# Layout of the compressed keys' and values' tokens in a hybrid attention block: one row of tokens and a shifted copy, or eight phases

## Chip, core and metric

The kernel runs on one core of a Trainium2 chip. The metric is the device time of one execution in microseconds (us), the median of several executions. The engines: PE (TensorE, matmuls; PEld is its weight load), DVE (VectorE), ACT (ScalarE), POOL (GpSimd), SP (SyncE, which here issues the transfers). A matmul below is written `out<-moving,stationary`.

## What is computed

One decoder layer on 512 tokens of width 1024: two attention branches side by side (differential attention, and sparse attention with compressed, selected and windowed keys), merged by gates, then an MLP. The change touches one step of the sparse branch, the compression of keys and of values:

```python
def compress(kv, pos_emb, w1, w2):            # kv: (1, 512, 4 groups, 64)
    n_cmp = (S - CMP_BLOCK) // CMP_STRIDE + 1 # 31 blocks of 32 tokens, 16 apart
    idx = jnp.arange(n_cmp)[:, None] * CMP_STRIDE + jnp.arange(CMP_BLOCK)[None, :]
    blocks = kv[:, idx] + pos_emb[None, None, :, None, :]
    blocks = blocks.transpose(0, 1, 3, 2, 4).reshape(B, n_cmp, G, CMP_BLOCK * Dh)
    return jax.nn.gelu(blocks @ w1) @ w2      # w1: (2048, 256), w2: (256, 64)
...
k_cmp = compress(kc.reshape(B, S, G, HEAD_DIM), cmp_pos_k[l], cmp_k_w1[l], cmp_k_w2[l])
v_cmp = compress(vc.reshape(B, S, G, HEAD_DIM), cmp_pos_v[l], cmp_v_w1[l], cmp_v_w2[l])
```

## The kernel before

**Tiling.** Every product is float32 made of parts: `split` writes a rounded high part (a cast on ACT or DVE) and a low part (a subtraction on DVE, for weights on DVE or POOL), and three matmuls (high by high, low by high, high by low) stand for one. Activations lie with 128 features or 128 tokens on the partitions; a PSUM bank is 128x512, and a chunk of a projection fills four banks (`gbanks`, four buffers named `gb`). Weights come in pieces of 128x1024 through `WStream`: a transfer into `wraw`, casts into `whi`, subtractions into `wlo`, each with two buffers.

**Order.** One generator, `filler`, walks the plan of matmul chunks (`add(...)`, lines 1556 to 1603): queries and keys of two differential heads, their values, `kc_chunk`, then `weave(diff_chunk(1, True), hidden(0))`, which alternates one weight piece of a projection with one piece of the compression's first layer for keys; then `diff_chunk(2)`, then `weave(dv_chunk(1, True), hidden(1))`, the same for values; and so on to the MLP. Streams for rotary embedding, scores and values of the attention heads run ahead of it in priority. All this only notes instructions. `Sched.flush` then gives each a place by a list schedule with prices and latencies written into the kernel, chooses for each cast or copy between ACT and DVE and for each weight subtraction between DVE and POOL, and emits the order of every engine at line 357, which is why each row below says L357. A change in one place so moves the order everywhere behind it.

**The step.** `kc_chunk` ends with `gb` banks that hold, for 512 tokens, the keys of groups 0 and 1, those of 2 and 3, and the values likewise. `u_split(0, ...)` splits the two key banks, 64 partitions (one group) at a time, into the lower half of the tile `U` (high and low, 2096 columns: four groups of 512 tokens and 48 columns of position embedding). One transfer then writes the upper half: the same columns one token further, so that a matmul contracts over two tokens of 64 features. The value banks are copied to a tile `kk`. In `hidden(kv)`, for each of two column tiles of w1 and each token pair `a` of 16, a matmul reads `U` from column 2a with a step of 16 (130 columns, high and low: 260), and one reads the high part alone (130). When `hidden(0)` is through, `u_split(1, ...)` does for the values what was done for the keys, into the next buffer of the same tag.

Of the kernel before, what the change touches and what calls it, by code (L numbers as in the profile page):

```python
# [11 lines left out]
F32 = mybir.dt.float32  # L12
F32R = mybir.dt.float32r
# [413 lines left out]
def hybrid_block(ctx: ExitStack, tc: tile.TileContext, x, ln_mix_g, w_in, dqg, dkg, lq1, lk1, lq2, lk2,  # L427
# [4 lines left out]
    V, A, P, T, Q = (Engine(sched, n, e) for n, e in (("DVE", nc.vector), ("ACT", nc.scalar), ("POOL", nc.gpsimd),  # L432
                                                      ("PE", nc.tensor), ("SP", nc.sync)))
# [3 lines left out]
    def pool(stack, name, space="SBUF"):  # L437
        kw = {} if space == "SBUF" else {"space": getattr(MT, space)}
        return Pool(sched, stack.enter_context(tc.tile_pool(name=name, bufs=1, **kw)), space)
# [10 lines left out]
    def f(ap):  # L450
        return ap.bitcast(F32)
# [4 lines left out]
    def copy(out, src, engs=("ACT", "DVE")):  # L456
        sched.note([(e, COPY[e], getattr(sched.engs[e], COPY[e])) for e in engs], (out, src), {})

    def tt(out, a, b, op, engs=("DVE",)):
        sched.note([(e, "tensor_tensor", sched.engs[e].tensor_tensor) for e in engs], (out, a, b), {"op": op})  # L460

    def split(hi, lo, src, hi_engs=("ACT", "DVE"), lo_engs=("DVE",)):

        copy(hi, src, hi_engs)
        tt(lo, src, f(hi), OP.subtract, lo_engs)
# [60 lines left out]
    def gemm_dm(banks, xs, nk=KT):  # L526

        for kp in range(nk // 2):
            hi, lo = ws.get()
            for a in range(2):  # L530
                kt = kp * 2 + a
                rh, rl = xs(kt)
                for c in range(4):
                    wh = hi[:, a * 512 + c * 128:a * 512 + (c + 1) * 128]
                    wl = lo[:, a * 512 + c * 128:a * 512 + (c + 1) * 128]
                    o = banks[c]
                    if len(rh.shape) == 3:
                        o = o.rearrange("p (t n) -> p t n", t=rh.shape[1])
                    mm(o, wh, rh, 512, kt == 0, False)
                    mm(o, wh, rl, 512, False, False)  # L540
                    mm(o, wl, rh, 512, False, kt == nk - 1)
                    yield 0
# [22 lines left out]
    with ExitStack() as ps:  # L565
# [5 lines left out]
        att = pool(ps, "att")  # L571


        def k_tile(dtype=F32R):
            return att.tile([128, 2, 2, 512], dtype, tag="kk", bufs=3, name="kk")
# [4 lines left out]
        UW = 2096  # L580
# [107 lines left out]
        def gbanks():  # L688
            return [pg.tile([128, 512], F32, tag="g", bufs=4, name="gb") for _ in range(4)]
# [11 lines left out]
        q_slots, k_slots, v_slots, r_slots = Slots(9), Slots(3), Slots(12), Slots(5)  # L701
# [12 lines left out]
        def there(key):  # L714
            if key not in ready:
                ready[key] = When(pe)
            return ready[key]


        U = [None, None]  # L720
        vcraw = [None]

        def u_split(kv, srcs):
            U[kv] = att.tile([128, 2, UW], F32R, tag="big", bufs=1, name="U")
            u = U[kv]

            pp = att.tile([128, 48], F32, tag="pp", bufs=1, name="pp")
            Q.dma_start(pp, (posk, posv)[kv])
            split(u[:, 0, 2048:], u[:, 1, 2048:], pp)
            for c in range(2):  # L730
                for g in range(2):
                    c0 = (c * 2 + g) * 512
                    split(u[0:64, 0, c0:c0 + 512], u[0:64, 1, c0:c0 + 512], srcs[c][g * 64:(g + 1) * 64])
            Q.dma_start(f(u[64:128, :, 0:2047]), f(u[0:64, :, 1:2048]))
            there(("U", kv)).after(9000)

        def kc_chunk():
            banks = gbanks()
            yield from gemm_dm(banks, hxs)
            u_split(0, banks[:2])  # L740
            yield k_slots.can(1)
            k_slots.take(1)
            vcraw[0] = k_tile(F32)[:, 0]
            for c in range(2):
                copy(vcraw[0][:, c, :], banks[2 + c])

        def hidden(kv):
            yield there(("U", kv))
            u = U[kv]
            w2r = att.tile([128, 2, 64], F32, tag="sc", bufs=2, name="w2r")  # L750
            Q.dma_start(w2r, (kw2, vw2)[kv][0].rearrange("(m p) n -> p m n", p=128))
            w2s = att.tile([128, 2, 2, 64], F32R, tag="pc", bufs=4, name="w2s")
            split(w2s[:, :, 0, :], w2s[:, :, 1, :], w2r)
            ghs = []
            for m in range(2):
                yield t_bank()
                hb = ptr.tile([128, 2, 256], F32, tag="t", bufs=2, name="hb")
                for a8 in range(2):
                    hi, lo = ws.get()
                    for aa in range(8):  # L760
                        a = a8 * 8 + aa
                        u2 = u[:, :, 2 * a:2 * a + 16 * 129 + 1:16]
                        c0 = aa * 128
                        mm(hb[:, :, 0:130], hi[:, c0:c0 + 128], u2, 260, a == 0, False)
                        mm(hb[:, 0, 0:130], lo[:, c0:c0 + 128], u2[:, 0, :], 130, False, a == 15)
                    if a8 == 1:
                        t_use(2000)
                    yield PIECE
                hs = att.tile([128, 130], F32, tag="sc", bufs=2, name="hs")
                copy(hs, hb[:, 0, 0:130])  # L770
                V.tensor_tensor(hs, hs, hb[:, 1, 0:130], op=OP.add)
                u_ = att.tile([128, 128], F32, tag="yt", bufs=2, name="hu")
                V.tensor_scalar(u_, hs[:, 0:128], hs[:, 128:129], None, op0=OP.add)
                t3 = att.tile([128, 128], F32, tag="ysq", bufs=2, name="t3")
                V.tensor_tensor(t3, u_, u_, op=OP.mult)
                V.tensor_tensor(t3, t3, u_, op=OP.mult)
                V.scalar_tensor_tensor(t3, t3, 0.044715, u_, op0=OP.mult, op1=OP.add)
                A.activation(t3, t3, AF.Tanh, scale=math.sqrt(2.0 / math.pi))
                V.tensor_scalar(t3, t3, 1.0, 0.5, op0=OP.add, op1=OP.mult)
                V.tensor_tensor(t3, t3, u_, op=OP.mult)  # L780
                gh = att.tile([128, 2, 128], F32R, tag="pc", bufs=4, name="gh")
                split(gh[:, 0, :], gh[:, 1, :], t3)
                ghs.append(gh)
            if kv == 0:
                u_split(1, [vcraw[0][:, c, :] for c in range(2)])
                k_slots.give(1)
            side.append(cmp_out(kv, ghs, w2s))

        def weave(main, sub):
# [349 lines left out]
        big = [None]  # L1139
# [504 lines left out]
```

## Time and profile before

| | |
|---|---|
| median of 3 executions | 1106.4 us (1106.22 to 1110.23) |
| the profiled execution | 1109.28 us |
| its span in the trace | 1107.5 us |
| PE busy | 1061.3 us, 96% |
| DVE / ACT / POOL busy | 769.9 / 462.0 / 490.3 us |
| granted TensorE clock, mean | 0.989 |

The span is what the trace covers; the profiled execution is 1.8 us longer, and 2.9 us above the median. Ends of matmuls in the trace are modelled and overlap, so the pace of PE is read from one start to the next. Busy shares are averages: up to about 700 us the attention streams run beside the projections, afterwards the MLP has PE nearly for itself.

### The profile page before, as it was taken

The page shows a single profiled execution, that of the slowest core. Times are in us where ns is not written, and L with a number is a line of the kernel's source. Part 1 is how long each engine was busy: PE and PEld are TensorE (multiplying, and loading weights), DVE is VectorE, ACT ScalarE, POOL GpSimd, SP SyncE. Part 2 cuts the span into 40 slices and gives each one's busy share as a digit, 9 for nine tenths or more (in the row PEclk, how much of TensorE's full clock was granted, in tenths as well). Part 3 has the DMA queues.
Part 4 walks back from the last instruction along what each step waited for, and adds up shares of the span by engine and source line. Part 5 has one row for each costly group of instructions (what it writes and reads, how often), then busy time and mean ns, then how long its engine had stood idle before and what let it go on. Part 6 is the DMA issues. An engine that isn't in the chain of part 4 may idle for free.

```text
span 1107.5 us, 15713 instructions
## 1 busy us (share of the span) xinstructions
PE 1061.3 (96%) x5257; PEld 881.4 (80%) x5257; DVE 769.9 (70%) x1899; ACT 462.0 (42%) x1125; POOL 490.3 (44%) x485
## 2 busy tenths in 40 slices
PE   6998988999999999998999997999999999999998
PEld 5877867788877788787788885888888888888887
DVE  7678498899888999999999897655543223345232
ACT  4256335566554556655465664213322111233110
POOL 3844698458687381392211213333333222333221
PEclk9999998999999999999999998999999999999999
DMA  6364345642645224454353243632232323332232
GB/s 207 96 171 109 109 128 145 160 149 69 172 121 159 75 66 155 121 189 165 117 178 124 96 153 113 228 105 79 93 103 100 102 96 95 96 95 96 95 133 76
DMA packets 83905, 136.76 MB, mean 123 GB/s; under 512 B 8817, under 2 KB 33905, under 8 KB 83825
## 3 DMA queue, kind: packets, MB, share of 16 engines
q1 hardware_dynamic: 83824, 135.77, 40.3%
q8 instruction: 41, 0.67, 0.2%
q14 instruction: 40, 0.32, 0.1%
HBM read 106.64 MB, written 14.42 MB: 109 GB/s over the span
## 4 chain that ended last, share of the span: by engine, by line
PE 74%; DVE 11%; DMA 6%; POOL 4%; issue 2%; SPq 1%; ACT 1%; DVEq 0%; ACTq 0%; POOLq 0%
PE gb L357 38%; PE ga L357 21%; PE sb L357 4%; PE avn L357 3%; PE ptn L357 3%; DMA kk<-kp 2%; DVE p L357 2%; PE hb L357 2%; POOL wlo L357 1%; PE av L357 1%; DVE st L357 1%; POOL str L357 1%; SPq L357 1%; DVE big L357 1%; POOL t1r L357 1%
## 5 line engine op out<-in xcount | busy, mean ns | idle before, releaser
L357 POOL TENSOR_TENSOR wlo<-wraw,whi 128x512 fp32r<-128x512 f32 (+1 forms) x214 | 305.3, 1436 | 523.4 <-ACT whi L357 350.2
L357 ACT CAST whi<-wraw 128x512 fp32r<-128x512 f32 (+1 forms) x213 | 127.6, 617 | 353.2 <-PE gb L357 172.6
L357 DVE CAST whi<-wraw 128x512 fp32r<-128x512 f32 (+1 forms) x101 | 45.8, 454 | 208.2 <-PE ga L357 96.1
L357 PE MATMUL gb<-wlo,hTh 128*128 128x512 f32 (+2 forms) x352 | 135.4, 386 | 2.8 <-POOL wlo L357 1.5
L357 PE MATMUL gb<-whi,hTl 128*128 128x512 f32 (+2 forms) x352 | 134.6, 383 | 0.0
L357 PE MATMUL gb<-whi,hTh 128*128 128x512 f32 (+2 forms) x352 | 131.1, 392 | 1.8 <-ACT hTh L357 1.2
L357 DVE CUSTOM_DVE_ANT_0 p<-sb,cst 128x512 f32<-128x512 f32 (+2 forms) x192 | 91.7, 480 | 9.6 <-PE sb L357 8.9
L357 DVE TENSOR_TENSOR wlo<-wraw,whi 128x512 fp32r<-128x512 f32 (+2 forms) x100 | 82.7, 828 | 4.8 <-ACT whi L357 0.7
L357 ACT ACTIVATE p<-p,smn 128x512 f32<-128x512 f32 (+3 forms) x128 | 71.9, 562 | 33.1 <-DVE smn L357 32.5
L357 PEld LDWEIGHTS gb<-wlo,hTh 128*128 128x128 f32 x352 | 67.4, 191 | 14.6 <-POOL wlo L357 3.1
L357 PEld LDWEIGHTS gb<-whi,hTh 128*128 128x128 f32 x352 | 67.4, 194 | 13.3 <-ACT hTh L357 1.6
L357 PEld LDWEIGHTS gb<-whi,hTl 128*128 128x128 f32 x352 | 67.3, 191 | 10.2 <-DVE hTl L357 0.3
L357 DVE TENSOR_SCALAR p<-p,smn,gates 128x512 f32<-128x512 f32 (+3 forms) x128 | 68.8, 546 | 0.9
L357 PE MATMUL gb<-big,whi 128*128 128x512 f32 x192 | 67.2, 404 | 0.0
L357 PE MATMUL gb<-hTl,whi 128*128 128x512 f32 x160 | 64.8, 405 | 0.0
L357 DVE TENSOR_TENSOR al<-ptn,ah 128x128 fp32r<-128x128 f32 (+3 forms) x128 | 61.0, 481 | 4.8 <-ACT ah L357 2.2
L357 PE MATMUL gb<-hTh,whi 128*128 128x512 f32 x160 | 64.3, 403 | 0.0
L357 PE MATMUL gb<-hTh,wlo 128*128 128x512 f32 x160 | 63.5, 404 | 0.0
L357 PE MATMUL ga<-h2l,whi 128*128 128x512 f32 x160 | 62.4, 390 | 0.0
L357 PE MATMUL ga<-h2h,whi 128*128 128x512 f32 x160 | 62.4, 391 | 0.0
L357 PE MATMUL ga<-h2h,wlo 128*128 128x512 f32 x160 | 62.3, 389 | 0.0
L357 PE MATMUL ptn<-cst,p 128*128 128x128 f32 x320 | 58.4, 276 | 2.3 <-DVE al L357 0.8
(246 smaller groups left out, 2634.7 us busy)
## 6 DMA issues: line engine op xcount, KB each, us to landing
wraw<-in_w_in_dram SPq DMA_DIRECT2D x36, 512.0 KB, 3.6
wraw<-in_w_mlp_up_dram SPq DMA_DIRECT2D x32, 512.0 KB, 3.9
wraw<-in_w_mlp_down_dram SPq DMA_DIRECT2D x32, 512.0 KB, 3.5
kk<-kp SPq DMA_DIRECT2D x48, 256.0 KB, 4.5
wraw<-in_w_in_dram SPq DMA_DIRECT2D x36, 256.0 KB, 4.1
big<-yd SPq DMA_DIRECT2D x16, 512.0 KB, 3.7
yd<-yo SPq DMA_DIRECT2D x8, 512.0 KB, 3.1
wraw<-in_w_proj_diff_dram SPq DMA_DIRECT2D x8, 512.0 KB, 3.9
```

Of the source, the lines that this page charges most:

```text
L357: op.ways[op.eng][0](*op.a, **op.k)
```

## The change

Both `U` tiles become one tile, `[128, keys or values, high or low, 8 phases of 130 columns]`. Token 16m + 2h + z of a group lies in phase h, column m of its group, and on the lower or upper 64 partitions by z. Sixteen copies (`kk<-gb`, 64 partitions, 8x32 elements) take the four banks out of PSUM into a tile `kk`, reading every sixteenth column of a bank; then casts and subtractions of 128x512 make `U` from `kk`, for keys and for values right behind each other. The matmuls of `hidden` read 130 neighbouring columns from column `a % 8 * 130 + a // 8`. The two transfers `U<-U`, the two whole-bank copies and the second `u_split` behind `hidden(0)` go, and the planner takes `U` for ready after 6000 instead of 9000 of its nanoseconds. The last columns of each part are set to zero.

```diff
-        U = [None, None]
-        vcraw = [None]
-
-        def u_split(kv, srcs):
-            U[kv] = att.tile([128, 2, UW], F32R, tag="big", bufs=1, name="U")
-            u = U[kv]
-
-            pp = att.tile([128, 48], F32, tag="pp", bufs=1, name="pp")
-            Q.dma_start(pp, (posk, posv)[kv])
-            split(u[:, 0, 2048:], u[:, 1, 2048:], pp)
-            for c in range(2):
+        U = [None]
+        UP = 130
+
+        def u_split(srcs):
+            ut = att.tile([128, 2, 2, 8 * UP + 4], F32R, tag="big", bufs=1, name="U")
+            U[0] = ut
+            V.memset(f(ut[:, :, :, 8 * UP:]), 0.0)
+            raw = k_tile(F32).rearrange("p a b n -> p (a b n)").rearrange("p (v h g m) -> p v h g m", v=2, h=8, g=4)
+            for k, src in enumerate(srcs):
+                kv, c = k // 2, k % 2
                 for g in range(2):
-                    c0 = (c * 2 + g) * 512
-                    split(u[0:64, 0, c0:c0 + 512], u[0:64, 1, c0:c0 + 512], srcs[c][g * 64:(g + 1) * 64])
-            Q.dma_start(f(u[64:128, :, 0:2047]), f(u[0:64, :, 1:2048]))
-            there(("U", kv)).after(9000)
+                    for z in range(2):
+                        sv = src[g * 64:(g + 1) * 64].rearrange("p (m h z) -> p z h m", h=8, z=2)[:, z]
+                        copy(raw[z * 64:(z + 1) * 64, kv, :, c * 2 + g, :], sv)
+            for kv in range(2):
+                u = [ut[:, kv, w, 0:8 * UP].rearrange("p (h n) -> p h n", n=UP) for w in range(2)]
+                pp = att.tile([128, 48], F32, tag="pp", bufs=1, name="pp")
+                Q.dma_start(pp, (posk, posv)[kv])
+                split(u[0][:, :, 128:], u[1][:, :, 128:], pp[:, 0:32:2].rearrange("p (z h) -> p h z", z=2))
+                rv = raw[:, kv].rearrange("p h g m -> p h (g m)")
+                for h in (0, 4):
+                    split(u[0][:, h:h + 4, 0:128], u[1][:, h:h + 4, 0:128], rv[:, h:h + 4])
+                there(("U", kv)).after(6000)
...
             yield from gemm_dm(banks, hxs)
-            u_split(0, banks[:2])
             yield k_slots.can(1)
             k_slots.take(1)
-            vcraw[0] = k_tile(F32)[:, 0]
-            for c in range(2):
-                copy(vcraw[0][:, c, :], banks[2 + c])
+            u_split(banks)
+            k_slots.give(1)
...
-            u = U[kv]
+            u = U[0][:, kv]
...
-                        u2 = u[:, :, 2 * a:2 * a + 16 * 129 + 1:16]
+                        at = a % 8 * UP + a // 8
+                        u2 = u[:, :, at:at + 130]
...
-            if kv == 0:
-                u_split(1, [vcraw[0][:, c, :] for c in range(2)])
-                k_slots.give(1)
```

What it moves on three engines is shown next. A number behind a name tells buffers apart.

PE, where the first piece of `hidden(0)` stands; `gb_341` to `gb_344` are the banks of `diff_chunk(1)`, `whi_314` its first weight piece, `whi_361` its second. Before:

```order
L357 MATMUL gb_344<-whi_314,hTl_69 128x512
L357 MATMUL av_354<-vt_234,ah_349 128x256
L357 MATMUL av_354<-vt_234,al_350 128x256
L357 MATMUL gb_341<-whi_361,hTh_68 128x512
L357 MATMUL gb_342<-whi_361,hTh_68 128x512
L357 MATMUL gb_343<-whi_361,hTh_68 128x512
L357 MATMUL gb_344<-whi_361,hTh_68 128x512
L357 MATMUL gb_341<-wlo_362,hTh_68 128x512
L357 MATMUL gb_341<-whi_361,hTl_69 128x512
L357 MATMUL gb_342<-wlo_362,hTh_68 128x512
L357 MATMUL gb_342<-whi_361,hTl_69 128x512
```

Now the banks are `gb_342` to `gb_345`, and the second piece is `whi_362`:

```order
L357 MATMUL gb_345<-whi_314,hTh_68 128x512
L357 MATMUL gb_345<-wlo_315,hTh_68 128x512
L357 MATMUL gb_345<-whi_314,hTl_69 128x512
L357 MATMUL hb_361<-U_338,whi_346 128x2x130
L357 MATMUL hb_361<-U_338,wlo_347 128x130
```

Before, ten matmuls of the second weight piece came first (two more follow the rows shown), then `hb`; now `hb` follows the first piece at once, two `av` matmuls have moved into its block of sixteen, and the second piece comes after it.

DVE, at the end of the step's work on `U` before that piece. Before:

```order
L357 SCALAR_TENSOR_TENSOR p_321<-p_331,sm_319,p_321 128x128
L357 TENSOR_SCALAR ys_303<-yt_326,sm_279 128x128
L357 TENSOR_TENSOR yt_336<-yt_336,av_335 128x128
L357 TENSOR_TENSOR U_338<-gb_243,U_338 64x512
L357 TENSOR_SCALAR sm_319<-sm_319 128x1
L357 TENSOR_TENSOR al_350<-pta_348,ah_349 128x128
L357 TENSOR_TENSOR yt_352<-yt_352,av_351 128x128
L357 TENSOR_SCALAR ys_303<-yt_336,sm_290 128x128
L357 CAST whi_361<-wraw_316 128x512
```

Now:

```order
L357 TENSOR_TENSOR U_338<-kk_339,U_338 128x4x128
L357 TENSOR_SCALAR ys_303<-yt_326,sm_279 128x128
L357 TENSOR_TENSOR U_338<-kk_339,U_338 128x4x128
L357 CAST U_338<-kk_339 128x4x128
L357 TENSOR_TENSOR U_338<-kk_339,U_338 128x4x128
L357 TENSOR_SCALAR ys_303<-yt_336,sm_290 128x128
L357 TENSOR_TENSOR al_351<-pta_349,ah_350 128x128
L357 TENSOR_TENSOR U_338<-kk_339,U_338 128x4x128
L357 TENSOR_TENSOR yt_353<-yt_353,av_352 128x128
L357 TENSOR_SCALAR sm_319<-sm_319 128x1
L357 TENSOR_TENSOR wlo_363<-wraw_316,whi_362 128x512
```

The two subtractions for the keys stand where the last one stood; those for the values follow, and behind them a weight subtraction in the place of a weight cast. From the banks' end to the second of these subtractions DVE's row holds six of the sixteen copies, one weight cast that stood on ACT, and two subtractions of 128x512; to the last subtraction shown of before it held two casts and four subtractions of 64x512. Over the whole program the planner gives DVE 110 weight subtractions of 128x512 instead of 98, and POOL 201 instead of 213; six of those that DVE gains stand before its 32nd softmax row of 192, four up to the last, one in the MLP.

SP, the queue of transfers at the same place. Before:

```order
L357 DMA yd0_70<-yo_329 128x1024
L357 DMA U_338<-U_338 64x2x2047
L357 DMA wraw_363<-in_w_in_dram 128x2x256 x2
L357 DMA wraw_366<-in_cmp_k_w1_dram 128x8x128
L357 DMA wraw_369<-in_w_in_dram 128x2x256 x2
```

Now:

```order
L357 DMA yd0_70<-yo_329 128x1024
L357 DMA wraw_364<-in_w_in_dram 128x2x256 x2
L357 DMA wraw_367<-in_cmp_k_w1_dram 128x8x128
L357 DMA wraw_370<-in_w_in_dram 128x2x256 x2
L357 DMA wraw_373<-in_cmp_k_w1_dram 128x8x128
```

The weight loads have moved up one place; the second `U<-U`, which stood further down between loads of `diff_chunk(2)`, is gone in the same way.

## Rows read from the trace of the kernel before

**Rows 1.** The page, part 1: busy time, share of the span, instructions of each engine.

```profile
PE 1061.3 (96%) x5257; PEld 881.4 (80%) x5257; DVE 769.9 (70%) x1899; ACT 462.0 (42%) x1125; POOL 490.3 (44%) x485
```

**Rows 2.** Chain of waits, 80 to 240 us: start, length, what.

```profile
103.07 7.29 DMA U<-U
...
128.14 2.69 POOL wlo L357 x2
```

**Rows 3.** PE timeline, 104.6 to 113.2: start, length, operation, idle before and releaser.

```profile
104.65 0.28 PE L357 MATMUL av<-vt,al 128*128 128x256 f32 x1
105.45 1.19 PE L357 MATMUL gb<-whi,hTh 128*128 128x512 f32 x4 [0.52 <-ACT whi L357]
107.12 0.50 PE L357 MATMUL gb<-wlo,hTh 128*128 128x512 f32 x1 [0.48 <-DVE wlo L357]
107.47 0.40 PE L357 MATMUL gb<-whi,hTl 128*128 128x512 f32 x1
...
108.41 0.39 PE L357 MATMUL gb<-whi,hTl 128*128 128x512 f32 x1
110.40 0.47 PE L357 MATMUL hb<-U,whi 128*128 128x260 f32 x1 [1.60 <-DMA U<-U]
110.69 0.29 PE L357 MATMUL hb<-U,wlo 128*128 128x130 f32 x1
110.80 0.40 PE L357 MATMUL hb<-U,whi 128*128 128x260 f32 x1
...
113.18 0.41 PE L357 MATMUL gb<-wlo,hTh 128*128 128x512 f32 x1
```

**Rows 4.** PE timeline, 86.6 to 87.2: first and last of four matmuls.

```profile
86.63 0.28 PE L357 MATMUL av<-vt,ah 128*128 128x256 f32 x1
...
86.98 0.28 PE L357 MATMUL av<-vt,al 128*128 128x256 f32 x1
```

**Rows 5.** Tile U: count, ns min/median/max, first and last start in us, forms.

```profile
L357 PE MATMUL hb<-U,whi x64: 381/403/515, 110.4 to 223.9; 128*128 128x260 f32 x64
...
L357 DVE TENSOR_TENSOR U<-gb,U x4: 678/688/694, 93.8 to 102.3; 64x512 fp32r<-64x512 f32 x4
...
DMA to landing us min/median/max: 7.0/7.1/7.3
```

**Rows 6.** DVE timeline, 90 to 112.

```profile
101.14 0.41 DVE L357 TENSOR_TENSOR al<-pta,ah 128x256 fp32r<-128x256 f32 x1
...
105.60 1.47 DVE L357 TENSOR_TENSOR wlo<-wraw,whi 128x512 fp32r<-128x512 f32 x1
```

**Rows 7.** Windows: PE, PEld, DVE, ACT, POOL busy (instructions), clock, DMA share, GB/s.

```profile
95.00:103.00 8.00, 7.20 (x44) 5.93 (x42) 7.84 (x24) 5.39 (x18) 3.61 (x5) 1.00 0.36 121
110.40:120.00 9.60, 9.60 (x50) 8.61 (x51) 2.61 (x6) 1.71 (x4) 3.19 (x2) 1.00 0.31 86
...
152.00:165.00 13.00, 11.68 (x44) 8.78 (x44) 11.73 (x21) 4.23 (x9) 12.36 (x16) 0.87 0.42 122
205.00:230.00 25.00, 23.31 (x133) 19.92 (x134) 22.06 (x70) 17.22 (x52) 12.35 (x15) 1.00 0.61 164
400.00:700.00 300.00, 286.01 (x1521) 236.88 (x1520) 274.64 (x772) 168.24 (x433) 98.64 (x84) 0.98 0.44 139
```

**Rows 8.** ACT and PE timelines near 150, with the releaser.

```profile
149.65 1.24 ACT L357 CAST whi<-wraw 128x512 fp32r<-128x512 f32 x2 [3.32 <-DMA wraw<-in_w_in_dram]
...
152.32 0.44 PE L357 MATMUL ptp<-cst,rw 128*128 128x128 f32 x2 [1.33 <-DVE o L357]
153.37 0.50 PE L357 MATMUL gb<-wlo,hTh 128*128 128x512 f32 x1 [0.62 <-POOL wlo L357]
```

**Rows 9.** Windows, 154 to 158, same columns.

```profile
154.00:156.00 2.00, 2.00 (x7) 1.54 (x6) 2.00 (x7) 0.00 (x0) 2.00 (x2) 0.59 0.76 215
156.00:158.00 2.00, 2.00 (x7) 1.42 (x5) 1.55 (x2) 1.05 (x2) 2.00 (x2) 0.56 0.13 51
```

**Rows 10.** The page, part 5: costliest groups, mean ns of one.

```profile
L357 DVE TENSOR_TENSOR wlo<-wraw,whi 128x512 fp32r<-128x512 f32 (+2 forms) x100 | 82.7, 828 | 4.8 <-ACT whi L357 0.7
```

## The prediction

> **What bounds the kernel now.** The page comes first: PE is busy 1061.3 us of 1107.5, no other engine above 70% [rows 1]. So what PE need not do, and what it need not wait for, is worth looking for; the page says nothing on where. The chain of waits says it for the stretch of the change: a transfer `U<-U` stands in it with 7.29 us from 103.07, and at 128.14 the chain goes over to POOL [rows 2]. PE's timeline then shows the transfer's price: between the last `av` at 104.65 and the first `hb` at 110.40, PE starts ten matmuls of 512 columns and otherwise stands still three times [rows 3]. The same timeline shows the second thing. A pair of `hb` matmuls, 260 and 130 columns, takes (113.18 - 110.80)/7 = 0.340 us from start to start, of which the 130 columns take 0.11 (110.69 to 110.80) [rows 3]. So 260 columns take 0.23. But 256 neighbouring columns take (86.98 - 86.63)/3 = 0.117 [rows 4], and 512 take (108.41 - 107.47)/4 = 0.235 [rows 3]. The 260 columns, read with a step of 16, run at half the pace.
>
> **The change, part by part.** The sum is made against the profiled execution, 1109.28 us, which lies 2.9 above the median.
>
> A. *Neighbouring columns in `hidden(0)`.* By the pace of 256 neighbouring columns, 260 take 0.117 x 260/256 = 0.119, so a pair falls from 0.340 to 0.23 and saves 0.11. The 130 columns alone gain nothing: 0.11 is what 128 or 256 columns take as well, so something other than columns sets it. There are 64 pairs [rows 5], 32 in each `hidden`: 3.5 us. From 110.4 to 120 PE is busy 9.60 of 9.60 us [rows 7], so here PE time is time. Taken: -3.5.
>
> B. *The first transfer.* PE could go on at 104.65 + 0.12 = 104.77, starts at 105.45; is through with four matmuls at 105.45 + 4 x 0.235 = 106.39, starts at 107.12; is through at 108.41 + 0.235 = 108.65, starts at 110.40: 0.68 + 0.73 + 1.75 = 3.2 us idle [rows 3]. In the new order `hb` stands right behind the first weight piece. Its eight pairs take 8 x 0.23 = 1.8 us, and the second piece's casts and subtractions, for which PE waited at 105.45 and 107.12, run beside them. All 3.2 go if `U` is there at 104.8. It is made by DVE, which is busy 7.84 of 8 us from 95 to 103 [rows 7]. Before, its part there is six instructions of 64x512, at 0.69 by the subtraction's row [rows 5]: 4.1 us, the last ending at 103.0. Now it is six copies of 256 elements, at 0.41 by a 128x256 instruction out of PSUM [rows 6], the moved weight cast and two subtractions of 512 elements, three more at 0.69 at most: 2.5 + 2.1 = 4.6. That gives 103.5, 1.3 us early. ACT has the other ten copies, and is busy 5.39 of 8 [rows 7]. Taken: -3.2; bounds -3.2 and 0.
>
> C. *Neighbouring columns in `hidden(1)`*: another 3.5, but PE is busy only 23.31 of 25 us there [rows 7], so 3.5 x 0.93 = 3.3. Taken: -3.3; bounds -3.5 and 0.
>
> D. *The second transfer* runs behind `hidden(0)` and lands 7.0 us or more after its issue [rows 5]. A weight load issued behind it keeps ACT waiting 3.32 us, to 149.65; PE then stands 1.33 + 0.62 = 1.95 us [rows 8], and right after that the granted clock is 0.59 and 0.56, near the lower of its two levels, for two slices of 2 us [rows 9]: 4 x (1 - 0.575) = 1.7 us of PE's work. Together 3.7. POOL, however, is busy 12.36 of 13 us from 152 to 165 [rows 7], and is what is late next. Half: -1.8; bounds -3.7 and 0. The 64x512 splits of the values, which went with the transfer, are made in A's place on engines that are nearly idle by 110 (DVE 2.61 of 9.60) [rows 7]; nothing for them.
>
> E. *Copies that read PSUM with a step of 16.* No row shows one. If they cost no more than neighbouring columns, nothing; if they are as much slower as the matmul's read (1.9 times), DVE has 6 x 0.41 x 0.9 = 2.2 us more, `U` is ready at 105.7 and PE waits 0.9. They cannot gain. Nearest is the plain 128x256 row, since the engines do not run at PE's pace; taken +0.3, bounds 0 and +2.2. A rule speaks against these copies: the Trainium skill, "Advanced Engine Details and Errata", section "Memory Cachelines", says that every two consecutive PSUM elements should be contiguous for best throughput. "Vector Engine (DVE) Microarchitecture Reference", section "Measured stream behaviour on trn2", of the Trainium skill, has 2.50 ns a column for a SBUF stream stepping 24 words against 1.05; by it, an estimate, six copies cost 2.2 us more and the sum 0.6 more. No row of this trace shows such a read.
>
> F. *The new order behind it.* DVE gets twelve weight subtractions that POOL had. Six fall into the weave, where DVE is nearly idle, one into the MLP; four into the attention stretch, where DVE is busy 274.64 of 300 [rows 7]. At 0.83 each [rows 10] they are 3.3 us; half of it on the path: +1.7. Below, since PE also stands 14 us in those 300 [rows 7] and a new order may fill some: bounds -4 and, with each at the 1.47 that one took at 105.60 [rows 6], +5.9.
>
> Sum: -3.5 - 3.2 - 3.3 - 1.8 + 0.3 + 1.7 = -9.8, so 1099.5 for a profiled run and 1096.6 for the median. Everything at its good end but F gives -13.9, or 1092.5; B at 0 and the rest as taken, 1099.8; the bad ends of D, E and F together, 1104.5.
>
> **Rivals.**
>
> *The gain waits for POOL.* The chain leaves PE at 128.14 [rows 2]. If POOL's work from there on cannot start earlier, the 6.7 us of A and B turn into waits before the next projections and only C, D, E and F are left: -3.1, or 1103. For: POOL is 95% busy from 152 to 165. Against: from 110.4 to 120 it is busy 3.19 of 9.60 [rows 7], so it has room, and it waits for PE's banks and weight buffers there.
>
> *It does not do what it says.* Columns for `a` of 8 and more start at an odd element. If such a read still takes 0.23, half of A and C is lost: 1100; if every one does, 1103.4. Nothing in the trace shows an odd start; the step alone explains the factor of two.
>
> *More than forecast.* D whole, F at -4: 1088.5 to 1092.
>
> *Slower: DVE becomes the bound.* Place: 400 to 700, where DVE is busy nine tenths [rows 7]. If scores and probabilities set the pace there whatever PE has gained, A to D become idle time of PE, and four weight subtractions at 1.47 put 5.9 us on DVE: 1112. It decides if the attention streams start no earlier than before, that is, if DVE's idle time before that grows by as much as PE gains. Against: DVE's idle stretch from 110 on is just the one that A and B shorten.
>
> **How the numbers follow.** Chances: the sum 0.60, with a range of its own of 1092 to 1103; the wait for POOL 0.17; the odd starts 0.06; more than forecast 0.08; slower by DVE 0.09. The likeliest gives 1096.6. To keep 8 in 10 the range takes in the two milder rivals and the good end nearly whole, and with F's bad end on the wait for POOL (1103 + 4): 1090 to 1108. What is left out is the slower rival and the far good end. A measurement of this kernel can tell about 0.5% (5.5 us) from no change: faster is below 1100.9. Of the sum's 0.60 some 0.48 lie there, with 0.08 of the better case and 0.07 of the two mild rivals: 0.63. Slower, above 1111.9, most of the last rival and a bad F: 0.08. The rest, 0.29, is the same.
>
> **What would show it.** A and C: `hb` pairs 0.23 apart. If they stay at 0.34, the layout is not what costs. B: no idle of PE between the last `av` of that piece and the first `hb`; if there is one, its releaser names DVE (copies or subtractions late) and E was too small. D: ACT no longer waits some 3 us for the weight load that lands near 149, and the clock stays at its upper level where it was 0.59. F: PE's busy share from 400 to 700 against 286 of 300, and DVE's time there. The wait for POOL: PE idle between 120 and 170 longer than before by as much as PE was earlier at 120. The prediction is wrong above all if the order behind 230, which is new from end to end, loses or wins more than F allows.

## The result, and the profile after

| | before | after |
|---|---|---|
| median | 1107.26 us (6 executions, 1106.22 to 1110.23) | 1097.22 us (6 executions, 1095.92 to 1099.06) |
| profiled execution / its span | 1109.28 / 1107.5 us | 1096.69 / 1094.9 us |
| PE / DVE / ACT / POOL busy | 1061.3 / 769.9 / 462.0 / 490.3 us | 1053.8 / 766.2 / 465.6 / 477.0 us |

The ratio is 0.9908, with a 95% interval of 0.9892 to 0.9923: 10.2 us faster. Forecast were 1096.6 us and 1090 to 1108. The sum came out right. Whether its terms did is what the experiments are for, and part of the answer is no.

PE's timeline of the changed kernel, where [rows 3] showed three waits between the last `av` and the first `hb` (start, length, operation, idle before and releaser):

```profile
104.17 0.39 PE L357 MATMUL gb<-whi,hTl 128*128 128x512 f32 x1
104.39 0.28 PE L357 MATMUL hb<-U,whi 128*128 128x260 f32 x1
...
104.57 0.34 PE L357 MATMUL hb<-U,whi 128*128 128x260 f32 x1
104.75 0.22 PE L357 MATMUL hb<-U,wlo 128*128 128x130 f32 x1
104.81 0.33 PE L357 MATMUL hb<-U,whi 128*128 128x260 f32 x1
...
106.05 0.39 PE L357 MATMUL av<-vt,ah 128*128 128x256 f32 x1 [0.44 <-DVE yt L357]
...
107.74 0.50 PE L357 MATMUL gb<-wlo,hTh 128*128 128x512 f32 x1 [0.16 <-DVE wlo L357]
```

The first `hb` follows the first weight piece with no gap, at 104.39 instead of 110.40. Pairs stand 0.24 apart here (104.57 to 104.81), 0.23 in the median, instead of 0.340. Of the 3.2 us of waits, 0.44 and 0.16 are left, now for DVE. The tiles `U` and `kk` (count, ns min/median/max, first and last start, forms) answer [rows 5]:

```profile
L357 PE MATMUL hb<-U,whi x64: 281/333/437, 104.4 to 218.0; 128*128 128x260 f32 x64
...
L357 ACT COPY kk<-gb x10: 354/367/370, 91.3 to 101.4; 64x256 f32<-64x256 f32 x10
L357 DVE COPY kk<-gb x6: 410/422/427, 92.1 to 100.5; 64x256 f32<-64x256 f32 x6
```

A DVE copy that reads PSUM with a step of 16 takes 0.422 us, where the plain 128x256 instruction of [rows 6] took 0.41. The windows answer [rows 7] (PE, PEld, DVE, ACT, POOL busy, granted clock, DMA share, GB/s):

```profile
104.80:120.00 15.20, 14.60 (x79) 12.29 (x79) 10.86 (x22) 4.87 (x13) 8.02 (x8) 1.00 0.41 118
152.00:165.00 13.00, 9.36 (x32) 6.61 (x31) 10.90 (x18) 5.54 (x10) 10.50 (x16) 0.74 0.67 172
400.00:700.00 300.00, 293.15 (x1557) 243.34 (x1556) 272.85 (x759) 169.99 (x436) 102.72 (x86) 0.99 0.46 145
```

From 104.8 to 120 DVE and POOL now work where they idled, as forecast. From 152 to 165 PE is busy 9.36 of 13 us at a mean clock of 0.74, where it had 11.68 at 0.87: a part of the gain is lost there. The low clock of [rows 9] is gone from its place, 154 to 158, but a longer stretch of it follows from 158 on (windows below). From 400 to 700 PE is busy 293.15 us instead of 286.01, in a stretch that the change does not touch.

To follow where time is won and lost, the time at which PE has started a given amount of matmuls is read in each trace (by its columns a matmul counts 0.227 us for 512, 0.119 for 256 or 260, 0.11 for 130 or 128), and that of the profiled execution of before taken off it. In us, negative is ahead; the kernels of the last three columns are told of below:

| PE's work, by before's time | after | step of 8 in the new order | three parts in the old order | new layout, slack 270 |
|---|---|---|---|---|
| 95.0 | -0.2 | -0.3 | -0.2 | +1.7 |
| 119.7 | -4.2 | -3.4 | -4.3 | -1.6 |
| 149.5 | -6.0 | -3.6 | -5.4 | -2.8 |
| 180.2 | -10.7 | -10.6 | -6.6 | -7.6 |
| 186.0 | -4.1 | -5.4 | -6.2 | -6.1 |
| 309.0 | -2.1 | -2.7 | -9.5 | -2.0 |
| 456.5 | -4.0 | -5.0 | -9.3 | +6.2 |
| 566.0 | -8.3 | -9.3 | -10.0 | +10.2 |
| 718.9 | -13.4 | -13.6 | -10.2 | +3.3 |
| 1098.6 | -12.7 | -13.4 | -9.8 | +3.4 |

Each column is a single execution, and that of before ran 2 us above its median, so a difference of 1 us in it says nothing. Executions of one kernel also differ with the clock that they were granted: of 26 of the kernel before, the three at a mean clock of 0.989 took 1107.8 to 1110.6 us, the three at 0.995 or more 1104.6 to 1106.9. But the curve of the changed kernel is not what the prediction's sum describes. It is 11 us ahead at 180, loses more than half of that within 6 us, is down to 2 at 309, and gets back 11 us by 719.

### The profile page after: what moved, and what is told of

The parts are those of the page before. It is cut to its first block, busy times and chain, and to the rows that moved or that the text cites. A ratio compares the mean times of both kernels' runs of the same rounds, so it can differ in the third digit from the quotient of the medians.

```text
span 1094.9 us, 15737 instructions
## 1 busy us (share of the span) xinstructions
PE 1053.8 (96%) x5257; PEld 875.6 (80%) x5257; DVE 766.2 (70%) x1905; ACT 465.6 (43%) x1136; POOL 477.0 (44%) x475
## 4 chain that ended last, share of the span: by engine, by line
PE 74%; DVE 12%; DMA 6%; POOL 4%; issue 2%; SPq 1%; ACT 1%; DVEq 0%; POOLq 0%; ACTq 0%
PE gb L357 38%; PE ga L357 22%; PE sb L357 4%; PE avn L357 4%; PE ptn L357 3%; DMA kk<-kp 3%; DVE p L357 2%; POOL str L357 1%; PE av L357 1%; POOL wlo L357 1%; SPq L357 1%; POOL t1r L357 1%; DVE al L357 1%; DVE sm L357 1%; DMA kk<-in_x_dram 1%
## 5 line engine op out<-in xcount | busy, mean ns | idle before, releaser
L357 POOL TENSOR_TENSOR wlo<-wraw,whi 128x512 fp32r<-128x512 f32 x203 | 289.0, 1432 | 522.7 <-ACT whi L357 396.2
L357 ACT CAST whi<-wraw 128x512 fp32r<-128x512 f32 (+2 forms) x217 | 130.0, 618 | 343.7 <-PE gb L357 167.0
L357 DVE CAST whi<-wraw 128x512 fp32r<-128x512 f32 x97 | 47.5, 489 | 199.7 <-PE ga L357 95.8
L357 PE MATMUL gb<-whi,hTh 128*128 128x512 f32 (+2 forms) x352 | 133.4, 388 | 1.5 <-ACT hTh L357 1.3
L357 DVE TENSOR_TENSOR wlo<-wraw,whi 128x512 fp32r<-128x512 f32 (+1 forms) x111 | 92.2, 832 | 7.2 <-ACT whi L357 2.7
L357 ACT CAST ah<-ptn 128x384 fp32r<-128x384 f32 (+3 forms) x98 | 41.2, 424 | 49.1 <-PE ptn L357 38.1
```

Of the source, the lines that this page charges most:

```text
L357: op.ways[op.eng][0](*op.a, **op.k)
```

## The experiments

All but the last four leave the planned order as it is in the kernel that they start from: the order is planned with the original operands, and only what is emitted differs (the diffs of these are shortened to that difference). Times are medians; gains in us are worked out from the ratios, with their 95% intervals (for a difference of two kernels, from both); the kernel before ran on the same chip as each group of runs, at 1107.98 (the first four), 1107.65 (the next four) and 1107.37 (the last four).

**The read step alone, in the new order.** The changed kernel with `hb` reading columns eight apart; other tokens are read.

```diff
-                        at = a % 8 * UP + a // 8
-                        u2 = u[:, :, at:at + 130]
+                        u2 = u[:, :, a % 8:a % 8 + 8 * 129 + 1:8]
```

> The kernel after, every engine's order as in it, but the matmuls of hidden read U with a step of 8 columns, so they take the wrong tokens (the compression's result is wrong, its work the same). Theory (neighbouring columns save PE time that stands on the path in both hidden stages): a pair of hb matmuls goes back to 0.34 us, the time comes out 5 to 7.5 us above the kernel after, near 1103, and most of the loss, 3.5 and about 3, is there at the ends of the two stages. Rival (PE's gain only turns into waits for POOL and DVE): pairs at 0.34 all the same, but no more than 2 us above the kernel after.

1097.76 us, ratio 0.992 (0.9899 to 0.9941), against 0.9908 for the changed kernel. The pairs are back at 0.34 (tile `U`):

```profile
L357 PE MATMUL hb<-U,whi x64: 381/398/469, 104.3 to 217.8; 128*128 128x260 f32 x64
```

and PE has lost 2.4 us of A's 3.5 by 149.5 in the table. At the end the step costs 0.5 us by the medians and 1.3 by the ratios, with room from -1.6 to 4.2. So A and C, 6.8 us in the prediction, are worth less than that in the order in which they were made; how much less these runs leave open. The clock had a part in it: four of the six executions with the step ran at a mean of 0.992 to 0.995 and took 1095.9 to 1097.9 us, two at 0.988 and 0.989 took 1102.0 and 1102.6; those of the changed kernel, at 0.989 to 0.992, took 1095.9 to 1099.1.

**The read step alone, in the old order.** The kernel before, `hb` reading 130 neighbouring columns (other tokens).

```diff
-                        u2 = u[:, :, 2 * a:2 * a + 16 * 129 + 1:16]
+                        u2 = u[:, :, a * 126:a * 126 + 130]
```

> The kernel before, every engine's order as in it, both transfers there, but the matmuls of hidden read 130 neighbouring columns of U (the wrong tokens; the compression's result is wrong). Theory: pairs of 0.23 us; 5 to 7 us below the kernel before, near 1101. The wait for the first transfer stays or grows a little. Rival (gain waits for POOL between 128 and 176): 2 to 3.5 us below, all of it from hidden(1).

1103.35 us, ratio 0.9967 (0.9953 to 0.9981): 3.7 us (2.1 to 5.2), of the 6.8 forecast. The pace is the same as in the changed kernel (281/333/388 ns for the 260 columns); about half of what PE saves reaches the end.

**Each transfer alone, in the old order.** The casts and subtractions of keys, or of values, write all 128 partitions, and that tile's `U<-U` is left out, so the upper half holds another group's features.

```diff
-                    split(u[0:64, 0, c0:c0 + 512], u[0:64, 1, c0:c0 + 512], srcs[c][g * 64:(g + 1) * 64])
-            Q.dma_start(f(u[64:128, :, 0:2047]), f(u[0:64, :, 1:2048]))
+                    split(u[:, 0, c0:c0 + 512], u[:, 1, c0:c0 + 512], srcs[c])
```

Keys:

> The kernel before, order as in it, the transfer U<-U for the keys left out; the splits of the keys write all 128 partitions instead of 64, in the same time (upper half of U holds other data, so the compression of keys is wrong). Step 16 stays. Theory (step B): PE no longer stands 1.75 us ahead of the first hb; the waits of 0.68 and 0.73 for the second weight piece stay, because hb stands behind them in this order. So 1.5 to 2 us below the kernel before, and the other 1.4 of step B came from the new place of hb. Rival (the stall is hidden by POOL's work later): within 1 us of before.

1104.86 us, ratio 0.9966 (0.9954 to 0.9978): 3.8 us (2.4 to 5.1), where 1.5 to 2 were expected. At the place itself the trace shows what was expected:

```profile
105.01 1.20 PE L357 MATMUL gb<-whi,hTh 128*128 128x512 f32 x4 [0.52 <-ACT whi L357]
106.70 0.50 PE L357 MATMUL gb<-wlo,hTh 128*128 128x512 f32 x1 [0.50 <-DVE wlo L357]
...
107.96 0.39 PE L357 MATMUL gb<-whi,hTl 128*128 128x512 f32 x1
108.19 0.38 PE L357 MATMUL hb<-U,whi 128*128 128x260 f32 x1
```

The first `hb` follows with no wait, 1.8 us less than in [rows 3], and the two waits for the second weight piece stay, since `hb` stands behind it in this order. They are 1.4 of B's 3.2 us, so this run is a test of the other 1.8 alone, and the end has 2 us more than that, which no run here explains. Values:

> The kernel before, order as in it, the transfer U<-U for the values left out in the same way (compression of values wrong). Theory (step D): the cast near 150 no longer waits 3 us for its weight load, PE's wait around 151 to 153 and the low clock at 154 to 158 are gone or shorter; 1.8 to 4.5 us below the kernel before (the kernel after was 3.6 us further ahead across that stretch). Rival (POOL is late there anyway): less than 1 us.

1106.31 us, ratio 0.9987 (0.9977 to 0.9997): 1.4 us (0.3 to 2.5), forecast 1.8 (D). Its windows answer [rows 9], and its PE timeline says why it is not the whole 3.7:

```profile
154.00:156.00 2.00, 1.58 (x8) 0.92 (x7) 1.30 (x4) 0.05 (x1) 2.00 (x3) 1.00 0.60 224
156.00:158.00 2.00, 1.07 (x5) 0.91 (x6) 1.97 (x3) 1.08 (x2) 2.00 (x3) 1.00 0.01 4
```

```profile
152.32 0.50 PE L357 MATMUL gb<-wlo,hTh 128*128 128x512 f32 x1 [1.48 <-POOL wlo L357]
...
156.93 0.51 PE L357 MATMUL gb<-wlo,hTh 128*128 128x512 f32 x1 [1.35 <-POOL wlo L357]
```

The clock stays at its upper level, 1.00 instead of 0.59 and 0.56, but PE now waits 1.48 and 1.35 us for POOL's weight subtractions. POOL is what was late next, as the prediction said. Matmul by matmul, the same order being planned, this execution is 0.5 us further ahead of before's behind this place (163) than in front of it (149.7). The rest of its lead comes later, where its clock is higher too (0.92 from 170 to 175, before 0.52).

**All three in the old order.** The three edits above together.

> The order of the kernel before, with all three direct parts at once: the first layer of the compression reads neighbouring columns, and both transfers U<-U are gone (the casts and subtractions write all 128 partitions instead, so the upper half holds another group's features instead of the shifted tokens). Alone the three parts gave 3.6 to 4.6 us, 3.1 to 3.7 and 1.4 to 1.7. Theory (in this order they add up, because each frees PE at another place): 8 to 10 us, 1098 to 1100, ratio 0.991 to 0.993; hb pairs 0.23 apart and no idle time of more than 0.5 us before the first hb. Rival (whichever of them comes first, the next wait for POOL or DVE takes the rest, as it took the neighbouring columns' gain in the order of the changed kernel): no better than the best two, 1101 to 1104. What is left between this and the changed kernel (1097.2) is then the new order by itself.

1099.89 us, ratio 0.9927 (0.9913 to 0.9942): 8.1 us (6.4 to 9.6). The single gains sum to 3.7 + 3.8 + 1.4 = 8.9. In this order they add up, and in the table the lead is kept from 309 on. The changed kernel's further 2.1 us (ratio 0.9908, intervals that overlap) would be its new order, the 1.4 us of B that hang on the new place of `hb` among them.

**What the read step costs.** The changed kernel with the step of `hb` set by hand (`m` is the column tile; for `m` of 1 the first matmul of a pair reads the 130 columns of the high part alone).

```diff
-                        u2 = u[:, :, at:at + 130]
+                        st = (2, 4, 8, 1)[a // 4] if m == 0 else 1 if a < 8 else 8
+                        u2 = u[:, :, a % 8:a % 8 + st * 129 + 1:st]
```

> The changed kernel with the columns that hb reads set by hand: in the first column tile of each hidden, a of 0 to 3 read with a step of 2, 4 to 7 of 4, 8 to 11 of 8, 12 to 15 neighbouring; in the second column tile the first matmul of a pair has the high part alone (130 columns instead of 260), for a of 1 to 7 neighbouring and for 8 to 15 with a step of 8. Other tokens are read, and part of the low half is left out. Read from it: the start-to-start time of a pair. With a step of 8 it was 0.34, neighbouring 0.233. If the step costs from 2 on, steps of 2 and 4 are at 0.34 too; if the distance in bytes counts up to the 32 of a step of 8, 2 and 4 lie at 0.23 or between. For the second question: if columns set the pace of a pair of neighbouring reads, 130 and 130 are through in 0.12 to 0.14; if the two weight loads set it, they stay at 0.22 to 0.24, and the prediction's 0.11 for any short matmul was right in kind.

The PE timeline, for a step of 2, of 8, for neighbouring columns, and for two neighbouring reads of 130 columns:

```profile
105.00 0.41 PE L357 MATMUL hb<-U,whi 128*128 128x260 f32 x1
105.23 0.30 PE L357 MATMUL hb<-U,wlo 128*128 128x130 f32 x1
105.35 0.42 PE L357 MATMUL hb<-U,whi 128*128 128x260 f32 x1
...
113.67 0.40 PE L357 MATMUL hb<-U,whi 128*128 128x260 f32 x1
...
114.00 0.40 PE L357 MATMUL hb<-U,whi 128*128 128x260 f32 x1
...
114.88 0.33 PE L357 MATMUL hb<-U,whi 128*128 128x260 f32 x1
...
115.11 0.33 PE L357 MATMUL hb<-U,whi 128*128 128x260 f32 x1
...
121.28 0.27 PE L357 MATMUL hb<-U,whi 128*128 128x130 f32 x1
121.39 0.27 PE L357 MATMUL hb<-U,wlo 128*128 128x130 f32 x1
121.50 0.28 PE L357 MATMUL hb<-U,whi 128*128 128x130 f32 x1
```

Start to start, a pair takes 0.35 with a step of 2 or 4, 0.33 with 8, 0.23 neighbouring. A step of 2 already costs all of it. A pair of 130 and 130 neighbouring columns takes 0.22 (121.28 to 121.50), hardly less than 260 and 130: two short matmuls in a row take 0.11 each, as the prediction had it. With a step of 8 the pair of 130 and 130 takes 0.22 too (206.71 to 206.93 neighbouring, 217.03 to 217.25 with the step).

**Where the new order lost the read step's gain.** The changed kernel, and the one with a step of 8, both with the weight subtractions of `diff_chunk(2)` and `dv_chunk(1)` cut to 8 columns: ten on POOL and six on DVE, fewer than the 25 that the expectation names. The matmuls that read `wlo` there read `whi`, so PE's work is the same.

```diff
                 self.split(hi[:, c], lo[:, c], self.raw[k][:, c], lo_engs=self.todo[k][1])
+                if k in self.left_out:
+                    op = self.sched.ops[-1]
+                    op.a = tuple(x[:, 0:8] for x in op.a)
+                    self.high[lo.tensor.name] = hi
...
         T.matmul(out, lhsT=lhsT, rhs=rhs, start=start, stop=stop)
+        if rhs.tensor.name in ws.high:
+            op, hi = sched.ops[-1], ws.high[rhs.tensor.name]
+            op.k = dict(op.k, rhs=hi[:, rhs.offset:rhs.offset + rhs.shape[-1]])
```

> The changed kernel with the subtractions for the weight pieces of diff_chunk(2) and dv_chunk(1) cut from 128x512 to 128x8; the matmuls that read wlo there read whi (so these two projections lose the weights' low part). Order and PE work as in the changed kernel; POOL and DVE have about 25 subtractions of 0.83 to 1.4 us less between 128 and 230 us. To be read against the same edit with a step of 8. Theory (what swallowed the neighbouring columns' 3 us between 150 and 186 is the wait for weight subtractions there): the stall of PE at 171 to 176 shrinks, and this kernel is 3 us or more ahead of the one with the step of 8 at the same PE work near 186. Rival (PE waits there for the rotary embedding and scores on DVE, whatever the weights): no more than 1 us ahead there. For the end: 1091 to 1096 if the time gained stays, 1096 to 1098 if later waits take it.

> The changed kernel with hb reading a step of 8 and with the same subtractions cut short (the same low parts left out). Theory: 3 us or more behind the version with neighbouring columns near 186 us, and 1.5 to 3.5 us behind it at the end. Rival: level with it near 186 and at the end, as the two full versions were (1097.8 against 1097.2).

1093.25 us, ratio 0.9862 (0.984 to 0.9883), and 1095.74, ratio 0.9894 (0.9874 to 0.9913): 2.5 us apart by the medians, 3.5 (0.3 to 6.8) by the ratios. Here the neighbouring columns are worth something at the end; that it is more than in the full pair (1.3, -1.6 to 4.2) the times alone do not show. The place shows in the PE timelines of the four kernels, each with the first matmul of the transposes that wait for DVE, and the next stall. The changed kernel, and with a step of 8:

```profile
157.46 0.70 PE L357 MATMUL ptp<-cst,rw 128*128 128x128 f32 x4 [2.76 <-DVE kp L357]
...
175.65 0.80 PE L357 MATMUL gb<-wlo,hTh 128*128 128x512 f32 x1 [1.82 <-DVE wlo L357]
```

```profile
158.28 0.63 PE L357 MATMUL ptp<-cst,rw 128*128 128x128 f32 x4 [1.55 <-DVE kp L357]
...
175.66 0.79 PE L357 MATMUL gb<-wlo,hTh 128*128 128x512 f32 x1 [1.82 <-DVE wlo L357]
```

The same two with the subtractions cut:

```profile
156.20 0.63 PE L357 MATMUL ptp<-cst,rw 128*128 128x128 f32 x4 [1.55 <-DVE kp L357]
...
171.21 0.39 PE L357 MATMUL av<-vt,ah 128*128 128x256 f32 x1 [0.67 <-ACT ah L357]
```

```profile
158.62 0.63 PE L357 MATMUL ptp<-cst,rw 128*128 128x128 f32 x4 [1.55 <-DVE kp L357]
...
174.65 0.39 PE L357 MATMUL av<-vt,ah 128*128 128x256 f32 x1 [0.68 <-ACT ah L357]
```

The order being the same, the two kernels of a pair can be compared matmul by matmul. Of the 3.3 us that A's 32 pairs save, 2.4 are there from 135 to 149.5; 0.8 went into the two waits behind the first eight pairs (0.44 and 0.16 in the timeline above; the kernel with a step of 8 has neither). In the full pair the longer wait (2.76 against 1.55) then leaves 0.82 us of the 2.4, and by 175.65 nothing; in the cut pair the waits are alike, and 2.4 us stay at 157 and 3.4 at 171. The rest of the loss stands in the windows of the changed kernel, and of the one with a step of 8:

```profile
154.00:156.00 2.00, 0.69 (x3) 0.21 (x2) 2.00 (x5) 1.73 (x4) 2.00 (x5) 1.00 0.65 236
156.00:158.00 2.00, 0.55 (x4) 0.42 (x4) 1.97 (x3) 0.00 (x0) 2.00 (x2) 0.97 0.00 0
...
160.00:162.00 2.00, 2.00 (x5) 1.61 (x6) 1.97 (x4) 1.96 (x4) 1.01 (x2) 0.50 0.99 238
```

```profile
154.00:156.00 2.00, 2.00 (x11) 1.63 (x11) 1.19 (x2) 1.17 (x3) 2.00 (x4) 1.00 0.68 181
156.00:158.00 2.00, 0.73 (x4) 0.24 (x2) 2.00 (x4) 1.40 (x3) 2.00 (x4) 1.00 0.21 81
...
160.00:162.00 2.00, 1.65 (x9) 1.19 (x8) 1.97 (x4) 1.95 (x4) 0.74 (x1) 1.00 0.97 190
```

The changed kernel's PE was busy 1.24 of these first 4 us and then works at half clock, 0.50, from 158 to about 164.7; the other keeps the upper level there. So in these two traces what had been won was given back first as a longer wait (from 2.4 us ahead to 0.8), then as clock (to 1.5 behind at 165); with the first nine pairs of `hidden(1)` they are level again at 171. From 175 to 182 the changed kernel has the lower clock once more (0.52 against 0.76), and at the end of these two traces it is 0.65 us behind: C is lost in them as well. The wait is what the cut removes. The clock is less certain a cause: in the cut pair it falls to 0.50 or 0.52 in both kernels near 160, behind the shorter wait, so that the two lose alike by it. That the wait hangs on POOL is in the chain of waits of the changed kernel (start, length, what), where POOL's own work stands from 123 to 150 and hands over to DVE:

```profile
145.58 2.08 POOL str L357
...
149.44 0.56 POOL st L357
150.00 0.03 issue
150.02 1.27 DVE o L357
```

and in the windows of the changed kernel and of the same with the subtractions cut, where POOL's busy time (the fifth engine) falls from 24.54 to 19.76 of 27 us:

```profile
123.00:150.00 27.00, 27.00 (x133) 22.58 (x132) 19.49 (x41) 11.09 (x24) 24.54 (x28) 1.00 0.33 98
```

```profile
123.00:150.00 27.00, 27.00 (x133) 22.57 (x132) 17.84 (x46) 11.25 (x24) 19.76 (x30) 1.00 0.40 118
```

**Other orders of the same work.** One number of the planner, the slack added to every latency between engines, set from 250 to 230 and to 270, in both kernels.

```diff
-SLACK = 250
+SLACK = 230      (and 270)
```

The new layout:

> The changed kernel, computed as it is, with one number of the planner changed: the slack that it adds to every latency between engines is 230 instead of 250 of its nanoseconds. The same work in another order from end to end; DVE has 111 weight subtractions, POOL 203, as in the changed kernel. Theory (an order that is merely another one is worth several microseconds either way, so the changed kernel's 2 to 3 us over its three direct parts say nothing of the layout): off the changed kernel's 1097.2 by 2 to 6 us, up or down. Rival (orders of the same work stay within 1.5 us, so the new order's gain belongs to the layout): 1095.7 to 1098.7.

> The changed kernel with the planner's slack at 270: DVE has 119 weight subtractions, POOL 195. Theory: off 1097.2 by 2 to 6 us, and if weight subtractions on DVE cost what the prediction gave them (half of 0.83 each), eight more of them on DVE weigh 3 us against it: 1099 to 1103. Rival: 1095.7 to 1098.7.

The layout of before:

> The kernel before with the planner's slack at 230: DVE has 107 weight subtractions, POOL 207 (before: 100 and 214). Theory: off the 1107.5 of before by 2 to 6 us, up or down; the step of 16 and both transfers are in it, so it stays above 1098. Rival (orders stay within 1.5 us): 1106 to 1109. Against the changed kernel with the same slack, the layout is worth 7 to 11 us if the direct parts hold in any order.

> The kernel before with the planner's slack at 270: DVE has 113 weight subtractions, POOL 201. Theory: off 1107.5 by 2 to 6 us. Rival: 1106 to 1109. Against the changed kernel with the same slack, the layout is worth 7 to 11 us if the direct parts hold in any order, and anything from 3 to 15 us if the order decides more than they do.

| slack | old layout | new layout | new less old |
|---|---|---|---|
| 230 | 1106.38, ratio 0.9988 (0.997 to 1.0005) | 1093.96, ratio 0.9881 (0.9866 to 0.9896) | -12.4 us |
| 250 | the kernel before | 1097.22, ratio 0.9908 (0.9892 to 0.9923) | -10.0 us |
| 270 | 1113.34, ratio 1.0052 (1.0032 to 1.0072) | 1112.82, ratio 1.0044 (1.0029 to 1.0058) | -0.5 us |

The rival, that orders of the same work stay within 1.5 us, is out: they spread by 18.9 us with the new layout and by 7.0 with the old (where a slack of 230 alone moved little). That the layout is worth 7 to 11 us in any order is out too. The fastest is the new layout with a slack of 230, 1093.96 us. The slowest of the new layout falls behind between 309 and 566 of the table, by 12 us, where the changed kernel gains 6. The page's chain by engine, of it and of the changed kernel:

```profile
PE 66%; DVE 17%; DMA 5%; POOL 5%; issue 3%; ACT 1%; SPq 1%; DVEq 0%; ACTq 0%; POOLq 0%
```

```profile
PE 74%; DVE 12%; DMA 6%; POOL 4%; issue 2%; SPq 1%; ACT 1%; DVEq 0%; POOLq 0%; ACTq 0%
```

and the windows of the two, 400 to 550:

```profile
400.00:550.00 150.00, 140.61 (x732) 115.92 (x731) 136.01 (x389) 78.20 (x204) 55.82 (x55) 0.95 0.43 128
```

```profile
400.00:550.00 150.00, 146.92 (x804) 122.02 (x803) 140.94 (x413) 88.69 (x229) 61.43 (x56) 1.00 0.46 144
```

More of its chain is DVE's, PE starts 72 matmuls fewer in these 150 us, and the clock is at 0.95. From 300 to 640 PE's waits sum to 13.4 us, 11.9 of them for DVE, against 5.4 in the changed kernel. The time is that of the prediction's slower rival, DVE as the bound in the attention stretch, but its mechanism is not shown: DVE is busy 136.01 us here and 140.94 in the faster kernel, which speaks for single DVE instructions that come late in this order, not for a DVE that is fuller. DVE has eight weight subtractions more than in the changed kernel (119 of 0.881 us, 104.7 in all, against 111 and 92.2 us); whether those 12.5 us have a part in it no run shows. With the old layout a slack of 270 loses 6 us too, which speaks for the order and not the layout.

## Why the prediction was right, and where it was not

**A and C, neighbouring columns (-3.5, -3.3).** The pace was right: 0.23 a pair. So was the reason, that 130 columns gain nothing since something else sets the 0.11; only the split within a neighbouring pair was off in the trace (0.17 and 0.06 from start to start, not 0.119 and 0.11). What failed is the step from PE's pace to the end. In the old order 3.7 of the 6.8 arrived, in the new one 1.3 (-1.6 to 4.2). Of A, 2.4 us were there at 149.5; 1.6 of them were then lost behind POOL's chain, and in the traced executions the rest to the clock. The prediction had this as a rival, "the gain waits for POOL", at 0.17, and read the evidence against it from 110 to 120, where POOL idles. What counted was POOL's work from 123 to 150, the chain that [rows 2] opens at 128.14. For C, the 0.93 was read from 205 to 230 [rows 7], but half of the pairs of `hidden(1)` run before 205, from 176.8 on, where the granted clock is 0.94; what became of C alone no run shows.

**B, the first transfer (-3.2).** Right. The kernel with a step of 8, which has B without A, is 3.1 us further ahead at 119.7 than at 95.0 in the table. In the changed kernel 0.6 us of waits came back, for DVE. `U`'s keys were through at 103.0, forecast 103.5. The transfer's part alone, in the old order, gave 3.8 (2.4 to 5.1) for the 1.8 us that it has in the sum; that surplus stays open.

**D, the second transfer (-1.8).** Right in size, 1.4 (0.3 to 2.5) alone. Its reason holds in part: without the transfer the clock at 154 to 158 came back, and POOL was late next. But the traces have 0.5 us of it at this place, and in the changed kernel the clock falls right behind it, from 158 on.

**E, copies with a step of 16 (+0.3).** Nothing: 0.422 us on DVE, 0.367 on ACT. The estimate from the Trainium skill's "Vector Engine (DVE) Microarchitecture Reference" (section "Measured stream behaviour on trn2"), 2.2 us more for six copies, does not hold for these reads of PSUM, nor does the rule of the Trainium skill's "Advanced Engine Details and Errata" (section "Memory Cachelines") show in them. The copies took what plain instructions of 256 elements out of PSUM took: 0.416 on DVE (`rw<-gb`), 0.373 on ACT (`ah<-pta`).

**F, the new order (+1.7, bounds -4 and +5.9).** The term that failed most, not by its size, which is inside its bounds, but as something that a sum can hold. Against the three parts in the old order the changed kernel is 2.1 us ahead by the ratios, with intervals that overlap (-0.2 to 4.5); 1.4 of that is B's, so F is -0.7 with 2.4 either way, and its sign is not settled. Against its own layout in two other orders the changed kernel is 3.3 behind and 15.6 ahead. The four weight subtractions that were costed at 3.3 us are not what decides it: the best order (slack 230) has as many on DVE, 111, as the changed kernel. The good end of the sum, -13.9, leaves F out; with F as taken it is -12.2, or 1094.2.

So the forecast 1096.6 met 1097.22 through two misses that cancel. What the old order could test, A to D without the 1.4 us of B's new place, was forecast at -10.4 and measured at -8.1 (-6.4 to -9.6). The rest, that 1.4 with E and F, was forecast at +0.6 and came out at -2.1 (-4.5 to 0.2). That they cancel is luck. The range held, but not for the reasons given: with a slack of 270 the same layout would have lain outside it, at 1112.8. Of the rivals, the odd starts are out (in the second block of eight `a`, all of which start one column on, pairs stand at 0.23 as well); the wait for POOL is seen for A alone; times towards "more than forecast" and at "slower by DVE" came up, 1093.96 and 1112.82, but from other orders.

What stays open: why the new order gains 11 us on the old between 309 and 719. In that stretch PE is busy 399.69 of 410 us at a mean clock of 1.00, before 392.88 at 0.99; so some 7 us are fewer waits and some 3 to 4, an estimate from the two clocks, the clock. No run changed that stretch alone.

## What to carry to other kernels

Where a planner sets the order from end to end, time an edit in several orders before believing its size: here one latency number moved the same work by 18.9 us, and the edit was worth 12.4, 10.0 or 0.5 us. Time saved on the bounding engine is worth what the next chain leaves of it; look for the next stretch in which another engine works almost without a break (here POOL, 24.54 of 27 us), and a lead can end there as a longer wait. For matmuls, lay moving columns next to each other where there are enough of them: 260 were read in half the time, 130 in the same 0.11 us. And before a difference of 1 or 2 us is put down to an edit, put the granted clock of the executions beside it.

## What was not expected of the hardware

- A moving operand read with a step of 2 is as slow as one with 4, 8 or 16: 260 columns at about 0.22 us instead of 0.12. There is no gentle start; and at 130 columns the step costs nothing (0.22 a pair of 130 and 130 either way).
- ACT and DVE read PSUM with a step of 16 at the pace of neighbouring elements (0.367 and 0.422 us for 64x256, against 0.373 and 0.416 for a plain 128x256).
- PE's granted clock fell to 0.50, the lower of its two levels, in the changed kernel after 4 us in which PE was busy 1.24 us (154 to 158), and stood there for 6 us or more: a PE that had come out of its wait 0.8 us earlier was 1.5 us behind at 165. With a step of 8 it stayed at 1.00 through the same place, and in both kernels with the cut subtractions it fell.
